# A hybrid decoder step on one core: TensorE's instructions issued strictly in the order of the source

## The chip, the cores and the metric

The kernel runs on one NeuronCore of a Trainium2 chip. The metric is the device time of one execution in microseconds. The kernel before takes 2900.02 us, the median of three runs.

## The reference

One inference step of a decoder of two layers, for 1104 tokens of width 1024: 16 meta tokens and 1024 prompt tokens of one sequence, and 8 sequences of 8 new tokens each with states of their own. All arithmetic is fp32.

```python
def trunk_layer(x, pos, lw, states, front_pad, chunk, attend):
    m, new_states = hybrid_mixer(rmsnorm(x, lw['g_pre_mix']), pos, lw, states, front_pad, chunk, attend)
    x = x + rmsnorm(m, lw['g_post_mix'])
    gate, up = jnp.split(rmsnorm(x, lw['g_pre_ffn']) @ lw['w_ffn_in'], 2, axis=-1)
    x = x + rmsnorm((jax.nn.silu(gate) * up) @ lw['w_ffn_out'], lw['g_post_ffn'])
    return x, new_states
```

`hybrid_mixer` multiplies the normed tokens by one input projection and hands its columns to three mixers: a gated DeltaNet (4 heads of 128 x 128 state, after a causal convolution of width 4), a Mamba-2 SSD scan (4 heads of 64, state 128), and sliding-window attention with sinks (4 query heads, window 128). Their outputs, 512 + 256 + 256 columns, are concatenated (`mixed`) and go through the output projection. The DeltaNet works in chunks: inside a chunk a triangular system is solved, and between chunks a state S is carried, in this recurrence:

```python
    def step(s, inp):
        u_c, w_c, attn_c, qd_c, kd_c, gl_c = inp
        v_new = u_c - jnp.einsum('bhcd,bhde->bhce', w_c, s)
        o_c = jnp.einsum('bhcd,bhde->bhce', qd_c, s) + jnp.einsum('bhij,bhje->bhie', attn_c, v_new)
        s = s * gl_c[..., None, None] + jnp.einsum('bhcd,bhce->bhde', kd_c, v_new)
        return s, o_c
```

## The kernel before

**Tiles.** The tokens lie in 9 tiles, eight of 128 and one of 80. Every dense product (input projection, output projection, feed-forward) is made of three fp16 matmuls: a weight slab `wsp` and the tokens (`xn`, `mixed` or `hsp`) are each split into a high and a low half, and high x high, high x low and low x high are added up in one PSUM bank (`mm3` and `mm3x`, lines 619 and 624). The loops run over layers, then over weight slabs or token tiles, then over 8 blocks of the contraction. The feed-forward takes part of its columns plainly and the rest by a product of 2 x 2 blocks with 7 instead of 8 multiplications.

**Stages of a layer.** Norm and transposes of the tokens (`norm_t`, line 586), the input projection, attention, SSD (`ssm_pre`, line 1844), the DeltaNet (`dn_inv`, line 1540, solves the triangular systems of four chunks at a time in two streams "0" and "1"; `dn_chain`, line 1680, is the recurrence; `dn_gate`, line 1794, gates its result into `mixed`), the output projection (in `dense`, line 831), the norm behind it with a second norm and its transposes (`out_post`, line 2026), and the feed-forward. All dense products of both layers are one generator, `dense`. Of the output projection, the three last tiles (6 to 8) are done in two parts, all heads but the last DeltaNet head first, with the part sums kept in DRAM; the tiles 0 to 5 are projected whole once the last head is done.

**The recurrence on the chip.** One chunk of `dn_chain` is a loop through three engines: a matmul of k and the state, `r` on VectorE (scalar_tensor_tensor out of PSUM), a matmul of `TF` and r, `y` on ScalarE (a copy out of PSUM), a matmul of `kd` and y, and the new state `S` on VectorE. Its matmuls are fp32; the trace shows each of them as two passes.

**`out_post`.** For a token tile it squares the projection's result `m` on ScalarE, multiplies m by a gain (VectorE or GpSimd, whichever the planner holds to be free first, `tt`, line 304), takes the root on GpSimd (`rqy`), adds to the residual `xt` on VectorE, stores it, and then does the same for the next norm, writing `m` again, whose eight 128 x 128 blocks TensorE transposes into the banks `tr` and `ch`. They are evicted into `xn2` for the feed-forward.

**What sets the order.** The source is one Python program in which each stage is a generator that yields where it must wait. The class `Plan` runs the generators. It wraps every engine (`engine`, line 206; the instruction itself is issued in line 214), and keeps a clock for each one. After each instruction `note` (line 155) adds the cost of a small table to that engine's clock:

```python
    HOP = {"T": 200.0, "V": 150.0, "S": 170.0, "G": 140.0, "D": 900.0}
    RATE = {"V": (1.04, 90.0), "S": (0.85, 55.0), "G": (2.1, 60.0)}
```

RATE is ns per column and a fixed part, HOP what is added before another engine may use a result; a matmul costs 0.42 ns (fp16) or 1.68 ns (fp32) per column and 3 ns. `run` (line 236) takes the first generator, by priority, whose operands are ready by that clock within 30 ns of TensorE's (`ready <= now + 30`), and emits its next instructions; the chains have priority 0, the inversions and norms 1, the dense products 9. So the source has a planned order of emission for all engines. PSUM is shared by tags: two banks `pd` and two `ps_inv`, two `ps_o`, one `ps_ch`, one `ps_tr`.

The emitted program then goes through the toolchain's scheduler. It keeps all dependencies, and chooses within them, by a timing model of its own, the order in which each engine issues; the order of emission is not binding for it. The number in an instruction's name is its place in the order of emission, so that the order on the chip can be laid beside it.

Of the kernel before, what the change touches and what calls it, by code (L numbers as in the profile page):

```python
# [110 lines left out]

NG = 23
NOW = -1.0


class Plan:
# [38 lines left out]
    def note(self, k, name, out, ins, acc, slow=False):  # L155
# [40 lines left out]
        if k != "D" or out.space != DRAM:  # L196
# [6 lines left out]
                L.append(b + (e + self.HOP[k],))  # L203
            self.last = max(self.last, e + self.HOP[k])

    def engine(self, eng, k):
        plan = self

        class E:
            def __getattr__(self, name):  # L210
                f = getattr(eng, name)

                def call(*a, **kw):
                    r = f(*a, **kw)  # L214
                    aps = [x for x in list(a) + [v for n, v in kw.items() if n not in ("out", "accum_out")]
                           if isinstance(x, bass.AP)]
                    out = kw.get("out")
                    if out is None:
                        out, aps = aps[0], aps[1:]
                    plan.note(k, name, out, aps, [kw["accum_out"]] if "accum_out" in kw else [],  # L220
                              kw.get("op") is ALU.pow)
                    return r

                return call

        return E()

    def mark(self, *keys):
        for key in keys:
            self.done[key] = self.last  # L230
# [5 lines left out]
    def run(self, *until):  # L236

        done = self.done
        while not until or any(k not in done for k in until):
# [31 lines left out]
            best[1], best[2] = self.last, None  # L271
            if r == NOW:
                best[1] = 0.0
# [8 lines left out]
def build(tc, A, depth=DEPTH):  # L282
    nc = tc.nc
    P = Plan()
    V, S, G, T, DQ = (P.engine(e, k) for e, k in ((nc.vector, "V"), (nc.scalar, "S"), (nc.gpsimd, "G"),
                                                 (nc.tensor, "T"), (nc.sync, "D")))
    dma = DQ.dma_start
    mark, done = P.mark, P.done
    es = ExitStack()
# [8 lines left out]
    def act(out, in_, func=AF.Copy, **k):  # L298
        S.activation(out=out, in_=in_, func=func, **k)
# [4 lines left out]
    def tt(out, a, b, op):  # L304

        n = 1
        for x in out.shape[1:]:
            n *= x
        t = {k: max(P.clk[k], P.clk["T"]) + P.RATE[k][0] * n for k in "VG"}
        (V if t["V"] <= t["G"] else G).tensor_tensor(out, a, b, op=op)  # L310
# [42 lines left out]
    def PS(tag):  # L353
        n = {"tr": 1, "inv": 2, "ch": 1, "o": 2}[tag]
        t = psm.tile([128, 512], F32, tag=tag, bufs=n, name="ps_" + tag)
        P.take(tag, n, t)
        return t
# [31 lines left out]
    def later(key, fn, n=0):  # L389

        def g():
            yield (key,)
            fn()
            free(n)
            mark((key, "st"))
        P.add(0, g())

# [13 lines left out]
    def load7(my, key, src):  # L411
# [11 lines left out]
        for k in range(4):  # L423
# [5 lines left out]
            def put(o, x):  # L429
                yield P.clk["V"]  # L430
                act(w[:, o, :512], x, scale=WS)
                stt(w[:, o, 512:], x, WS, w[:, o, :512], MUL, SUB)
# [20 lines left out]
            mark(key + (k,))  # L453
            yield NOW

# [6 lines left out]
    def loader():  # L462
        while True:
# [31 lines left out]
            if key[0] == "w2" and key[2] == 0:  # L495
# [3 lines left out]
                split[0] += 1  # L499
                yield NOW  # L500
                continue
# [29 lines left out]
            mark(key)  # L531
            yield NOW

# [52 lines left out]
    def norm_t(xt, C, i, gb, dst, xs, tag, halves=False):  # L586
# [6 lines left out]
        for hf in range(2):  # L593
# [13 lines left out]
            V.tensor_tensor(lo, pc, hi, op=SUB)  # L607
            yield NOW if hf == 0 else None

# [19 lines left out]
    def dense_ws(p, w, xn, g):  # L629

        g0, gn = g
        for kt in range(8):
            mm3(p[:, :gn], w[:, 0, kt * 128:(kt + 1) * 128], w[:, 1, kt * 128:(kt + 1) * 128],
                xn[:, kt, 0, g0:g0 + gn], xn[:, kt, 1, g0:g0 + gn], kt == 0, kt == 7)
            if kt < 7:
                yield NOW

# [1622 lines left out]
def make(arrays, depth=DEPTH):  # L2260
    import concourse.bacc as bacc

    nc = bacc.Bacc("TRN2", target_bir_lowering=False, num_devices=1)
    A = {n: nc.dram_tensor(n, a.shape, mybir.dt.from_np(a.dtype), kind="ExternalInput").ap()
         for n, a in arrays.items()}
    for n, s in OUTS.items():
        A[n] = nc.dram_tensor(n, s, F32, kind="ExternalOutput").ap()
    with tile.TileContext(nc) as tc:
        build(tc, A, depth)
    return nc  # L2270
# [9 lines left out]
```

## Time and profile before

| | us |
|---|---|
| median of 3 runs (2899.88 to 2901.44) | 2900.02 |
| the profiled execution | 2895.58 |
| its span, first to last instruction | 2893.5 |
| mean granted clock of TensorE in it | 0.981 |
| busy: TensorE / its weight loads | 2743.2 / 1909.5 |
| busy: VectorE / ScalarE / GpSimd | 1933.3 / 1288.4 / 813.1 |

The profiled execution is one execution with the hardware profiler on; 2.08 us of its time lie outside the span. Engines are named PE (TensorE's matmuls), PEld (its weight loads, which run beside the matmuls), DVE (VectorE), ACT (ScalarE), POOL (GpSimd) and SP (the queue of DMA issues). A busy time is the time in which at least one instruction of the engine runs. Nearly every instruction has the line 214, since the planner's wrapper issues it; so groups are told apart by the program's names, out<-in. The granted clock is a share of TensorE's full 2.4 GHz.

### The profile page before, as it was taken

What the parts mean: (1) busy time and instruction counts of PE and PEld (TensorE: products, weight loads), DVE (VectorE), ACT (ScalarE), POOL (GpSimd) and SP (SyncE); (2) the same over time, 40 slices, a digit from 0 to 9 for tenths busy, and PEclk for the clock granted to TensorE, in tenths of its full rate; (3) what the DMA queues carried; (4) which work ended last, traced back from release to release, by engine and by line L of the source; (5) the groups of instructions that cost most, each with busy time, mean ns of one, the idle gap of its engine ahead of it and who ended that gap; (6) DMA issues with size and microseconds to landing.
All of it is one profiled execution on the core that took longest, in us unless ns stands there. A gap on an engine that the chain in (4) does not pass through costs nothing. (4 is left out here: it accounts for less than half of the span.)

```text
span 2893.5 us, 50019 instructions
## 1 busy us (share of the span) xinstructions
PE 2743.2 (95%) x19662; PEld 1909.5 (66%) x19662; DVE 1933.3 (67%) x3614; ACT 1288.4 (45%) x3015; POOL 813.1 (28%) x1124
## 2 busy tenths in 40 slices
PE   6999999999799999999899999999998999999997
PEld 3766677664588888744348676777646888886443
DVE  5557667655757676767865676666457666766776
ACT  5435456554423333433544455655543333334342
POOL 2204523313543333200260062223136233231011
PEclk8999999999899999999999999999999999999998
DMA  5011110132301111242431111001222111113333
GB/s 183 31 60 37 57 38 31 38 104 89 109 30 59 53 51 59 96 120 68 163 128 34 50 47 46 31 31 56 86 103 87 50 54 59 52 52 110 106 115 124
DMA packets 74092, 209.79 MB, mean 73 GB/s; under 512 B 13360, under 2 KB 24816, under 8 KB 73824
## 3 DMA queue, kind: packets, MB, share of 16 engines
q1 hardware_dynamic: 73856, 206.59, 21.8%
q8 instruction: 154, 2.52, 0.4%
q14 instruction: 82, 0.67, 0.1%
HBM read 175.49 MB, written 33.04 MB: 72 GB/s over the span
## 5 line engine op out<-in xcount | busy, mean ns | idle before, releaser
L214 PEld LDWEIGHTS <-wsp 128*128 128x128 f16 x10704 | 1044.1, 99 | 305.7 <-issue 12.9
L214 PE MATMUL pd<-xn,wsp 128*128 128x336 f16 (+3 forms) x4512 | 737.7, 311 | 3.4 <-DVE a L214 3.1
L214 DVE SCALAR_TENSOR_TENSOR wsp<-raw,wsp 128x512 f16<-128x512 f32 (+2 forms) x414 | 404.8, 986 | 196.3 <-ACT wsp L214 193.5
L214 ACT ACTIVATE wsp<-raw 128x512 f16<-128x512 f32 (+2 forms) x414 | 311.0, 763 | 393.5 <-DVE raw L214 145.9
L214 PEld LDWEIGHTS <-hsp 128*128 128x128 f16 x1848 | 182.1, 99 | 242.0 <-issue 30.2
L214 PE MATMUL pd<-wsp,hsp 128*128 128x512 f16 x924 | 232.6, 385 | 17.1 <-ACT wsp L214 11.8
L214 PE MATMUL ps_o<-wsp,hsp 128*128 128x512 f16 x924 | 230.7, 383 | 0.5 <-DVE m L214 0.5
L214 PE MATMUL pd<-wsp,mixed 128*128 128x512 f16 (+1 forms) x864 | 212.0, 384 | 5.8 <-DVE m L214 5.8
L214 POOL TENSOR_SCALAR rqy<-ss 128x1 f32<-128x1 f32 (+1 forms) x72 | 56.1, 779 | 551.1 <-ACT jk L214 407.6
L214 DVE SCALAR_TENSOR_TENSOR u<-R,lp_cw,u 128x512 f32<-128x512 f32 x216 | 180.0, 869 | 4.3 <-ACT u L214 3.4
L214 ACT ACTIVATE hsp<-hid 128x512 f16<-128x512 f32 x154 | 89.8, 620 | 180.4 <-PE ps_o L214 143.7
L214 PE MATMUL pd<-wsp,xn 128*128 128x512 f16 (+3 forms) x864 | 161.2, 338 | 6.0 <-ACT wsp L214 3.4
L214 PE MATMUL ps_o<-xn,wsp 128*128 128x256 f16 (+1 forms) x1296 | 165.1, 285 | 0.0
L214 POOL TENSOR_TENSOR raw<-raw 128x512 f32<-128x512 f32 x74 | 95.5, 1292 | 241.9 <-DVE raw L214 208.4
L214 PE MATMUL ps_inv<-xn,wsp 128*128 128x256 f16 (+1 forms) x1248 | 154.0, 281 | 0.8 <-DVE a L214 0.8
L214 POOL TENSOR_TENSOR U<-U,hid 128x256 f32<-128x256 f32 (+1 forms) x114 | 80.3, 733 | 239.3 <-ACT hid L214 239.3
L214 PEld LDWEIGHTS <-mixed 128*128 128x128 f16 (+1 forms) x864 | 84.4, 101 | 82.4 <-issue 11.3
L214 DVE TENSOR_TENSOR hsp<-hid,hsp 128x512 f16<-128x512 f32 x154 | 101.4, 684 | 43.3 <-ACT hsp L214 43.3
L214 PEld LDWEIGHTS <-xn 128*128 128x128 f16 (+1 forms) x864 | 87.4, 103 | 55.9 <-issue 10.7
L214 PE MATMUL ps_ch<-xn,wsp 128*128 128x296 f16 x456 | 109.2, 289 | 0.0
L214 PE MATMUL ps_tr<-xn,wsp 128*128 128x256 f16 x456 | 108.6, 273 | 0.0
L214 DVE TENSOR_TENSOR W<-ps_inv,c 128x512 f16<-128x512 f32 (+1 forms) x120 | 71.0, 595 | 46.3 <-PE ps_inv L214 45.4
(496 smaller groups left out, 4738.9 us busy)
## 6 DMA issues: line engine op xcount, KB each, us to landing
raw<-wfi SPq DMA_DIRECT2D x88, 512.0 KB, 3.5
raw<-wfo SPq DMA_DIRECT2D x70, 512.0 KB, 3.7
raw<-wf SPq DMA_DIRECT2D x44, 512.0 KB, 3.3
xd<-xt SPq DMA_DIRECT2D x24, 512.0 KB, 2.9
xt<-xd SPq DMA_DIRECT2D x24, 512.0 KB, 5.7
xt<-x SPq DMA_DIRECT2D x16, 512.0 KB, 6.1
raw<-wo SPq DMA_DIRECT2D x16, 512.0 KB, 3.4
tcx<-wfo SPq DMA_DIRECT2D x10, 512.0 KB, 3.7
```

The lines of the kernel that those rows point to most:

```text
L214: r = f(*a, **kw)
```

## The change

The planner gets a method `keep`, which is called with each instruction that the wrapper has just issued and its engine's letter. For the letters in `PINNED`, here "T" alone, it hands the instruction to the toolchain's `keep_in_program_order`, which puts it in issue order behind the instruction of the same engine that was handed over before it. The edge holds inside one engine's queue: it adds no semaphore and no instruction. TensorE's 18392 matmuls and transposes are so issued in the order of emission. The other engines' instructions are ordered by the scheduler as before, with TensorE's order given.

```diff
--- before.py
+++ after.py
@@ -111,6 +111,7 @@
 
 NG = 23
 NOW = -1.0
+PINNED = "T"
 
 
 class Plan:
@@ -203,6 +204,10 @@
                 L.append(b + (e + self.HOP[k],))
             self.last = max(self.last, e + self.HOP[k])
 
+    def keep(self, k, ins):
+
+        return self.pin(ins) if k in PINNED else ins
+
     def engine(self, eng, k):
         plan = self
 
@@ -211,7 +216,7 @@
                 f = getattr(eng, name)
 
                 def call(*a, **kw):
-                    r = f(*a, **kw)
+                    r = plan.keep(k, f(*a, **kw))
                     aps = [x for x in list(a) + [v for n, v in kw.items() if n not in ("out", "accum_out")]
                            if isinstance(x, bass.AP)]
                     out = kw.get("out")
@@ -282,6 +287,7 @@
 def build(tc, A, depth=DEPTH):
     nc = tc.nc
     P = Plan()
+    P.pin = tc.keep_in_program_order
     V, S, G, T, DQ = (P.engine(e, k) for e, k in ((nc.vector, "V"), (nc.scalar, "S"), (nc.gpsimd, "G"),
                                                  (nc.tensor, "T"), (nc.sync, "D")))
     dma = DQ.dma_start
```

## Rows read from the trace of the kernel before

**Rows 1.** The page, part 1: busy us, share of the span, instructions.

```profile
PE 2743.2 (95%) x19662; PEld 1909.5 (66%) x19662; DVE 1933.3 (67%) x3614; ACT 1288.4 (45%) x3015; POOL 813.1 (28%) x1124
```

**Rows 2.** Waits of TensorE, whole span: us in total, times, longest us.

```profile
PE ps_tr L214 <- DVE m L214: 31.2, 15, 6.7
```

**Rows 3.** Windows, all engines: window, us, busy (count) by engine, PEclk, DMA share, GB/s.

```profile
10.00:75.00 65.00, 47.28 (x244) 26.33 (x242) 35.22 (x56) 32.96 (x77) 21.84 (x36) 0.84 0.48 162
647.00:683.10 36.10, 33.18 (x200) 20.90 (x198) 16.14 (x49) 14.69 (x57) 10.27 (x15) 1.00 0.19 61
1398.80:1493.40 94.60, 81.77 (x388) 38.34 (x388) 79.68 (x100) 46.95 (x78) 35.56 (x44) 0.97 0.48 154
```

**Rows 4.** TensorE's timeline at the chain's end: start us, us, what it did.

```profile
656.34 0.59 PE L214 MATMUL pd<-wsp,mixed 128*128 128x512 f16 x2
656.77 0.44 PE L214 MATMUL ps_ch<-r,TF 128*128 128x128 f32 x2
...
672.69 0.38 PE L214 MATMUL pd<-wsp,mixed 128*128 128x512 f16 x1
...
681.00 2.32 PE L214 MATMUL pd<-wsp,mixed 128*128 128x512 f16 x10
```

**Rows 5.** Tiles y and r, whole span: duration in ns, min/median/max.

```profile
L214 PE MATMUL ps_ch<-y,prep x144: 270/275/377, 403.0 to 2100.9; 128*128 128x128 f32 x128, 16*128 16x128 f32 x16
...
L214 ACT ACTIVATE y<-ps_ch x72: 254/277/322, 402.5 to 2100.4; 128x128 f32<-128x128 f32 x64, 80x128 f32<-80x128 f32 x8
...
L214 DVE SCALAR_TENSOR_TENSOR r<-ps_ch,nE,prep x80: 332/348/353, 401.6 to 2099.2; 128x128 f32<-128x128 f32 x64, 64x128 f32<-64x128 f32 x8, 16x128 f32<-16x128 f32 x8
```

**Rows 6.** Timelines of VectorE and GpSimd, 748 to 765 us.

```profile
755.06 3.36 DVE L214 SCALAR_TENSOR_TENSOR xt<-m,rqy,xt 128x1024 f32<-128x1024 f32 x1 [2.10 <-POOL rqy L214]
...
761.52 1.28 DVE L214 SCALAR_TENSOR_TENSOR m<-xt,rqy,gpf 128x1024 f32<-128x1024 f32 x1 [0.72 <-POOL rqy L214]
...
754.98 2.35 POOL L214 TENSOR_TENSOR m<-m,gpo 128x1024 f32<-128x1024 f32 x1
```

**Rows 7.** Windows, tile pd alone: window, us, busy (count) of PE, DVE, ACT, PEclk, ...

```profile
647.00:683.10 36.10, 15.32 (x53) 0.00 (x0) 1.68 (x4) 1.00 0.19 61
2070.40:2106.50 36.10, 15.33 (x53) 0.00 (x0) 1.67 (x4) 1.00 0.19 61
450.20:465.20 15.00, 7.61 (x37) 0.00 (x0) 0.55 (x3) 1.00 0.11 37
```

**Rows 8.** TensorE's timeline around the output projection's end and after.

```profile
752.01 1.75 PE L214 MATMUL ps_o<-xn,wsp 128*128 128x256 f16 x8
...
759.07 1.56 PE L214 MATMUL pd<-wsp,mixed 128*80 128x512 f16 x6 [2.92 <-DVE m L214]
...
763.41 0.75 PE L214 MATMUL ps_tr<-c,m 128*128 128x128 f32 x4
...
781.42 0.37 PE L214 MATMUL pd<-xn,wsp 128*128 128x256 f16 x1 [3.15 <-DVE a L214]
784.65 1.09 PE L214 MATMUL ps_tr<-c,m 128*128 128x128 f32 x4 [2.86 <-DVE m L214]
```

**Rows 9.** Groups by form, TensorE, 752.0 to 784.6 us: busy, mean, idle before.

```profile
L214 PE MATMUL ps_o<-xn,wsp 128*128 128x256 f16 x48 | 8.1, 335 | 0.0
L214 PE MATMUL pd<-xn,wsp 128*128 128x256 f16 x49 | 6.3, 275 | 3.1 <-DVE a L214 3.1
L214 PE MATMUL ps_inv<-xn,wsp 128*128 128x256 f16 x48 | 5.4, 272 | 0.0
```

**Rows 10.** TensorE's timeline at the start of an inversion.

```profile
607.54 2.97 PE L214 MATMUL pd<-wsp,mixed 128*128 128x512 f16 x13
611.20 0.40 PE L214 MATMUL ps_inv<-c,Mh 128*128 128x128 f16 x4 [0.69 <-ACT Mh L214]
```

**Rows 11.** Windows, all engines, columns as in rows 3: the clock after two waits.

```profile
2203.90:2210.70 6.80, 2.64 (x13) 2.34 (x14) 5.38 (x7) 3.45 (x7) 2.43 (x4) 0.52 0.60 202
...
760.10:763.50 3.40, 3.40 (x17) 2.31 (x16) 2.59 (x3) 1.89 (x4) 3.13 (x4) 0.53 1.01 334
```

## Prediction

> **What bounds the kernel now.** I read the page first: TensorE is busy for 2743.2 of the span's 2893.5 us [rows 1]. It is the bound over the run, and the 150.3 us in which it stands idle are what an order of its instructions can add to or take from. Next came the list of what it waits for: transposes that wait for a VectorE result `m` lead with 31.2 us in 15 waits, the longest of 6.7 us [rows 2]. The reader should see that no single wait is large: the leading kind is a sum of short pauses.
>
> Then I put two orders side by side: the one in which the source emits the matmuls, and the one in which the program before has them. Of 18392 matmuls 2472 stand elsewhere, none by more than 101 places: 1110 further forward, 1362 further back. The displaced ones form 92 closed stretches. In them 949 dense matmuls (a weight slab as one operand) run ahead of work that the source emits first; their spacings add up to 189 us. I sorted the idle time before each matmul the same way: 13.6 us of it ends at one that was moved forward, 58 us at one moved back, 67 us at one that was not moved. So little of today's waiting is the fault of a matmul that went too early, and the dense work moved forward mostly fills time in which the earlier work was not ready.
>
> The page's rows by window say the same for the stretches that matter [rows 3]: TensorE is busy for 33.18 of 36.10 us at the end of the DeltaNet chain, and for 81.77 of 94.60 us between the layers. The timeline shows how: in the chain's end each step of the recurrence (S, r, y) leaves TensorE a pause, and two dense matmuls sit in it [rows 4].
>
> **What the change does to that.** It adds no work on any engine and no wait between engines; it takes away the freedom to fill. A matmul whose operands are late now holds up everything emitted behind it. How late they are follows from the source: the planner emits a step where its own cost table says that it is ready. The table gives 109 + 55 = 164 ns for the 128-column copy to y on ScalarE, the row says 277; 133 + 90 = 223 ns for r on VectorE, the row says 348 [rows 5]. It gives VectorE's 1024-column pass 1155 ns, and the row shows 3.36 us where GpSimd's pass on m runs beside it [rows 6]. So the emitted order is too early for the steps that wait, and TensorE pays the difference. Four places in each layer, named by layer 0:
>
> *Chain end, 647.0 to 683.1 us.* The output projection of the first tiles is emitted only when the planner has the last head's result, behind the whole chain. Its first matmuls need the other three heads alone, so the program before runs 53 of them here (the only tile pd has in this window, and 53 again in layer 1) [rows 7]. Ten of them in a row take 2.32 us [rows 4]; less the 0.38 that one takes to drain this is 0.216 each, so 11.4 us of work moves behind the chain. The chain itself gains little: its steps start within 0.1 us of their operands already. I take 10.5 us. Ends: 8.5 if the 2.9 us of idle time here go as well; 16 if the emptier stretch runs at half clock (the 48 chain passes of the y, r and S kinds at 0.377 instead of 0.275 us [rows 5] add some 5).
>
> *Output projection to FFN, 752 to 789 us.* The source emits the transposes of tile 5 right behind the projection of tile 6, which ends at 752.0; they start at 763.41 [rows 8], because the VectorE and GpSimd passes in front of them end only then [rows 6]. Before, dense matmuls of the FFN go in between. Up to the transposes of tile 7 at 784.65 [rows 8], 144 of them have run (48 + 49 + 48 [rows 9], less the one after the 3.15 us wait); the source emits 72 ahead of these transposes. The other 72 at 0.1125 us (5.4 us for 48) are 8.1 us. Besides, tile 7's projection moves from between 752.0 and 759.07 to behind 764 [rows 8], and its eviction on VectorE by up to 6.5 us; most of that is absorbed by VectorE's queue, I add 1. Taken: 9. Ends: 2 if the 3.15 and 2.86 us of waiting there [rows 8] vanish; 15 if the delay passes on in full.
>
> *Two inversion streams, 450 to 488 us.* 62 matmuls of 384 columns are moved forward, 37 of them before 465 [rows 7]. At 0.164 us (384 at the rate of 512 columns in 0.216) that is 10.2 us. Two streams cover part of each other's waits, so I take 4; ends -1.4 (the idle time of the stretch) and 10.2.
>
> *Start of an inversion, 605 to 614.5 us.* The source has it wait for Mh, which is there at 611.2; 13 dense matmuls fill the time now [rows 10]. By the two orders 27 are moved forward here, 5.8 us. I take 4; ends -0.7 and 5.8.
>
> The smaller stretches of a layer hold another 91 such matmuls, 15 to 20 us at these spacings, with some 7 us of idle time. There the source is early by a fraction of a microsecond at a time and the filler comes right behind; I take 0, with ends -7 and 20. Four places in two layers: 2 x (10.5 + 9 + 4 + 4) = 55 us.
>
> Once only: between the layers (1398.8 to 1493.4) 90 matmuls, 22 us, are moved forward and 12.8 us are idle [rows 3]. VectorE is busy for 79.68 of 94.60 us, so it sets the pace either way: 5 us, ends -11 and 22. At the end of layer 1, 35 matmuls, 9 us: 2 us, ends 0 and 9. In the first 75 us, 88 matmuls, 19 us at full clock, stand against 65.00 - 47.28 = 17.7 us of idle time [rows 3]; loads and the norm chain hold both orders up: 0, ends -18 and 19.
>
> The sum is 55 + 5 + 2 + 0 = 62 us. The profiled execution takes 2895.58 us, its span 2893.5; 62 on top give 2957.6. It lies 4.4 us under the median of 2900.02, so against the median I forecast 2962 us. VectorE, ScalarE, GpSimd and the DMA queue keep their instructions; what they do later they do because a matmul came later, and that is inside the terms above.
>
> **The clock.** After the 2.92 us wait of 759 us the granted clock is 0.53 for a stretch of 3.4 us, after the 6.7 us wait of layer 1 it is 0.52 for 6.8 us [rows 2, 8, 11]: the lower level, 1.2 GHz, after an idle TensorE. The long waits that I expect stand where such drops already are, so the sum has nothing for it and the upper end holds it. The Trainium skill, "TensorE: Matmul & The Clock Gate", section "Loop structure matters more than you think", says that waits between matmuls let the array fall to the slow clock and that dense work should follow without gaps. By that rule three new long waits per layer would each cost some 2 to 3 us more of slow matmuls, an estimate from the page's two rates, and the sum would be near 78 instead of 62. By that rule the drops behind the waits of 2.92 and 6.7 us are what it describes, and these rows agree with it.
>
> **Rivals.** *Faster:* the five pauses that end at a matmul moved forward go, 13.6 us together, among them the one of 3.15 us at 781.4 [rows 8] and four of 1.4 to 3.4 us at the start and between the layers; the late chains lose the dense matmuls in front of them. That is 2886 us. It decides if the fill lost in the four places stays under 13.6 us, less than a quarter of what I count. For it speaks that the start and the seam between layers are such places; against it, that 53 matmuls alone are 11 us per layer. Chance 0.12.
>
> *Half of it:* the toolchain orders the other engines anew around the fixed TensorE order, so that VectorE and GpSimd serve the waiting transposes first; the pass of 3.36 us next to GpSimd's [rows 6] shows that there is room. Then the chain end (21 us) and a little more remain: 2926 us. Chance 0.20.
>
> *No change:* the edges order only what was in order, or gains at the seams and losses in the chains cancel: 2900 us. 2472 displaced matmuls speak against the first. Chance 0.10.
>
> *More:* every filler is lost and the clock falls as well, 2 x (16 + 15 + 10 + 6) = 94, with the seams, start and end over 100: above 3000 us. Chance 0.05.
>
> **How the numbers follow.** The forecast, 2940 to 3000 with 2962 in it, has 0.53. A measurement of this kernel can tell about 0.2%, 5.8 us, from no change. Slower by more: 0.53 + 0.20 + 0.05 = 0.78; within: 0.10; faster: 0.12. The range 2894 to 3000 leaves out the faster case and the one above, 0.17 together.
>
> **What would show it.** In the changed profile the chain's end should hold no matmul of the output projection, with TensorE busy for some 22 us instead of 33.18. The transposes of m should lead the list of waits with pauses near 10 us at tile 5, and a pause of about 4 us should stand before the first matmul on Mh. TensorE's idle time should come to about 212 us, its busy time stay within 10 us of 2743. If the idle time falls, or the transposes of m wait less, the forecast is wrong in its direction; if it grows only at the chain's end, it was half of it.

## The result, and the profile after

The changed kernel takes 3014.53 us (median of 4 runs, 3011.94 to 3018.61) against 2899.95 us (4 runs): a ratio of 1.0398, 95% interval 1.0385 to 1.0411, slower by 114.6 us. The direction of the forecast holds; the time does not. 2962 was forecast, and 3014.53 lies above the range's end of 3000.

The page after, part 1, answers to [rows 1]:

```profile
PE 2782.6 (92%) x19662; PEld 1940.3 (64%) x19662; DVE 1933.8 (64%) x3614; ACT 1291.6 (43%) x3015; POOL 818.3 (27%) x1124
```

Its span is 3010.1 us, 116.6 more than before. TensorE executes the same instructions, yet is busy for 39.4 us more (2782.6 against 2743.2), and stands idle for 3010.1 - 2782.6 = 227.5 us, 77.2 more than the 150.3 of before. Those are two losses, and the split is the main reading of this case. The mean granted clock went from 0.981 to 0.960. As the clock has two levels, full and half, these means stand for about 110 us at half clock before and about 241 us after, an estimate from the two spans.

Where they arise is seen by taking points at which both kernels have executed the same set of matmuls, and comparing the windows between them. Ten such windows, five in each layer, hold 99.1 of the 116.6 us. Here are those of layer 0 and the sum over all ten, first of the kernel before (the chain's end is in [rows 3]; columns as there, the sum line has the ten windows' lengths first):

```profile
450.20:487.70 37.50, 36.10 (x318) 28.06 (x316) 25.63 (x62) 24.03 (x70) 9.92 (x19) 1.00 0.13 44
505.80:548.20 42.40, 39.17 (x318) 27.30 (x316) 29.26 (x58) 22.76 (x53) 10.64 (x21) 0.96 0.16 52
605.00:611.40 6.40, 5.71 (x38) 3.10 (x37) 4.99 (x8) 2.21 (x3) 1.27 (x2) 1.00 0.52 165
...
751.40:788.70 37.30, 28.02 (x201) 22.10 (x200) 31.00 (x33) 15.16 (x29) 23.20 (x24) 0.84 0.39 130
...
sum 319.40, PE 283.91 PEld 202.91 DVE 213.79 ACT 157.95 POOL 110.75; mean PE 28.39 PEld 20.29 DVE 21.38 ACT 15.79 POOL 11.08
```

And of the kernel after:

```profile
451.10:496.40 45.30, 41.69 (x313) 33.52 (x313) 25.40 (x62) 23.98 (x68) 9.85 (x18) 0.81 0.10 36
514.70:562.70 48.00, 41.11 (x318) 28.94 (x317) 30.63 (x59) 22.74 (x53) 10.84 (x19) 0.89 0.14 46
620.40:630.80 10.40, 7.00 (x37) 3.96 (x38) 7.52 (x11) 3.26 (x4) 1.28 (x2) 0.84 0.57 182
666.80:722.30 55.50, 42.67 (x195) 26.94 (x195) 19.16 (x53) 17.02 (x58) 10.09 (x15) 0.78 0.21 71
790.20:836.40 46.20, 29.41 (x202) 22.33 (x201) 34.55 (x45) 18.28 (x37) 31.62 (x31) 0.76 0.29 98
...
sum 418.50, PE 327.17 PEld 233.65 DVE 242.14 ACT 172.61 POOL 131.70; mean PE 32.72 PEld 23.36 DVE 24.21 ACT 17.26 POOL 13.17
```

The count behind TensorE's busy time hardly changes from one to the other (318 and 313 entries in the first window), the busy time does, and the clock column says why. In the ten windows TensorE is busy for 327.17 - 283.91 = 43.3 us more and idle for 55.8 us more. Place by place, each growth as busier + idler:

| place | layer 0 | layer 1 | taken in the sum |
|---|---|---|---|
| two inversion streams | 7.8 = 5.6 + 2.2 | 6.5 = 4.1 + 2.4 | 4 |
| 505.8 to 548.2 us | 5.6 = 1.9 + 3.7 | 5.3 = 1.6 + 3.7 | 0 |
| start of an inversion | 4.0 = 1.3 + 2.7 | 5.3 = 2.6 + 2.7 | 4 |
| chain's end | 19.4 = 9.5 + 9.9 | 21.2 = 11.2 + 10.0 | 10.5 |
| projection to feed-forward | 8.9 = 1.4 + 7.5 | 15.1 = 4.1 + 11.0 | 9 |

Outside them the seam between the layers adds 5.4 us and the end of layer 1 4.7 us. The first 75 us end 0.8 us later, after a detour: 9.0 us are lost there and won back.

The leading wait of TensorE is the same as before [rows 2], and the one that is now second has grown from 10.9 to 23.0 us (columns as there):

```profile
PE ps_tr L219 <- DVE m L219: 42.8, 14, 11.3
PE ps_tr L219 <- DVE xt L219: 23.0, 4, 9.1
```

Its two longest stand where the forecast put "pauses near 10 us at tile 5". The one in layer 0, in the timeline (start us, us, what it did):

```profile
787.97 0.60 PE L219 MATMUL ps_ch<-c,m 128*128 128x128 f32 x4
788.40 2.63 PE L219 MATMUL pd<-wsp,mixed 128*128 128x512 f16 x6
801.20 1.08 PE L219 MATMUL ps_tr<-c,m 128*128 128x128 f32 x4 [10.17 <-DVE m L219]
```

### The profile page after: what moved, and what is told of

The parts are those of the page before. It is cut to its first block, busy times and chain, and to the rows that moved or that the text cites. A ratio compares the mean times of both kernels' runs of the same rounds, so it can differ in the third digit from the quotient of the medians.

```text
span 3010.1 us, 50030 instructions
## 1 busy us (share of the span) xinstructions
PE 2782.6 (92%) x19662; PEld 1940.3 (64%) x19662; DVE 1933.8 (64%) x3614; ACT 1291.6 (43%) x3015; POOL 818.3 (27%) x1124
## 5 line engine op out<-in xcount | busy, mean ns | idle before, releaser
L219 PE MATMUL ps_tr<-xn,wsp 128*128 128x256 f16 x456 | 108.6, 273 | 0.0
```

Of the source, the lines that this page charges most:

```text
L219: r = plan.keep(k, f(*a, **kw))
```

## The experiments

All start from the changed kernel. Each was timed beside the kernel before on the same chip; the table has the difference of the medians, and, from its profiled execution, TensorE's busy and idle time (the span less the busy time) and its mean granted clock.

| run | median us | to before | busy | idle | clock |
|---|---|---|---|---|---|
| before | 2900 | 0 | 2743.2 | 150.3 | 0.981 |
| changed | 3014.5 | +114.6 | 2782.6 | 227.5 | 0.960 |
| two_orders | 2923.3 | +25.6 | 2744.2 | 176.2 | 0.979 |
| free_out | 2951.9 | +51.4 | 2755.0 | 193.5 | 0.973 |
| free_inv | 2973.2 | +74.4 | 2768.9 | 204.0 | 0.968 |
| early | 3013.2 | +115.6 | 2770.6 | 239.9 | 0.960 |
| load | 3003.5 | +103.0 | 2778.3 | 220.6 | 0.964 |
| early_load | 2972.3 | +71.7 | 2767.2 | 206.7 | 0.966 |
| dummy | 3024.1 | +126.4 | 2796.5 | 226.0 | 0.964 |
| dummy2 | 3009.1 | +108.6 | 2791.8 | 218.0 | 0.967 |
| hop | 3002.1 | +104.5 | 2768.7 | 229.2 | 0.962 |
| all_pinned | 3014.5 | +115.7 | 2780.3 | 232.9 | 0.956 |
| early_load_free | 2892.8 | -6.0 | 2745.2 | 147.3 | 0.978 |
| early_free | 2902.7 | +3.2 | 2747.0 | 153.0 | 0.979 |

**Which order costs.** In `two_orders` the ordering edges tie dense matmuls only to dense ones and the rest only to the rest:

```diff
-    P.pin = tc.keep_in_program_order
+    prev = {}
+
+    def pin(ins):
+        side = P.cur == "dense"
+        if side in prev:
+            tc.add_manual_dep(ins.ins, prev[side].ins.name, mybir.DependencyInfo(
+                mybir.DependencyClass.NoSync, mybir.DependencyReason.DATA), reason="keep_in_program_order")
+        prev[side] = ins
+        return ins
+
+    P.pin = pin
```

(`P.cur` is the name of the generator that the planner runs.)

> The dense matmuls keep the source's order among themselves, and all other TensorE instructions keep it among themselves, but the one kind is free against the other. If the 114.6 us are lost because dense work may no longer run ahead of chains and transposes (the theory), nearly all of it comes back: 2895 to 2925 us. If the loss lies in the order of the chains, inversions and transposes among themselves (the rival), it stays above 2960 us.

2923.26 us: 89 of the 114.6 us come back. TensorE's busy time is within 1 us of the kernel before, the clock at 0.979: with the dense work free, the whole of the clock's loss is gone. The 25.6 us that stay are idle time (176.2 against 150.3); the order inside either kind is all that is still bound.

**Is the loss where the windows say?** Two runs bind everything but the dense matmuls of one stage: `free_out` those from the part sums of the output projection to the first plain products of the feed-forward, `free_inv` those from the DeltaNet's projections to the part sums.

```diff
+    def pin(ins):
+        if P.free and P.cur == "dense":
+            return ins
...
+            P.free = True
             part = range(NT - NPT, NT)
```

> Order of the source everywhere, but the dense matmuls from the output projection to the first plain products of the feed-forward are free against the rest. By the growth of the changed kernel between common points (19.4 and 21.1 us at the chain's end, 8.9 and 13.6 us from the output projection to the feed-forward) the theory expects 63 us back, 2947 to 2957 us. If the loss is spread by something else than these places (the rival), above 2980 us.

> Order of the source everywhere, but the dense matmuls from the DeltaNet's projections to the part sums of the output projection are free against the rest; those of the output projection's whole tiles and all later ones are bound. By the growth of the changed kernel between common points in the inversions (18.9 and 19.7 us from the first chain to the last head) the theory expects 39 us back and some 2 us per layer more from the last tile's part sums, 2970 to 2978 us. If the inversions are late by their own order against the chain and not by the lost fill (the rival), over 2995 us.

2951.93 and 2973.15 us: 63.2 and 40.2 us come back (the four runs of `free_inv` lie between 2961.86 and 2976.87). The sum, 103.4 of 114.6 us, counts one place twice: the dense matmuls at the start of an inversion are part sums of the output projection, which both runs leave free, and the 4.0 and 5.3 us lost there are gone in both. So some 94 us come back from distinct places, against 99.1 in the ten windows; in `free_out` the chain's end still loses 3.9 and 3.8 us. The freed matmuls are not tied to one another either. The pages, part 1, of `free_out` and of `free_inv`:

```profile
PE 2755.0 (93%) x19662; PEld 1930.3 (65%) x19662; DVE 1934.6 (66%) x3614; ACT 1290.6 (44%) x3015; POOL 814.4 (28%) x1124
```

```profile
PE 2768.9 (93%) x19662; PEld 1925.4 (65%) x19662; DVE 1930.4 (65%) x3614; ACT 1289.3 (43%) x3015; POOL 820.6 (28%) x1124
```

Of the busy time 27.6 us come back in the one and 13.7 in the other, 41.3 together, where 39.4 were lost; of the idle time 34.0 and 23.5. Here too the start of an inversion is counted in both.

**What the filler in the chain is worth.** Here the order stays bound and the source is changed: it emits the three-heads part of the first tile's projection before it asks for the last head (not shown: `dense_tok` gets two arguments, so that one call can begin a sum and a later one finish it).

```diff
+            yield tuple(("mix", l, h, 0) for h in range(3)) + (("ssm", l, 0), ("swa", l, 0))
+            early = []
+            for hf in range(2):
+                early.append(pd())
+                yield from dense_tok(early[hf], mx, wo[hf * 4:hf * 4 + 4], 0, 512, (0, 1, 2, 4, 5, 6, 7), True, False)
+                yield NOW
             yield room(2)
...
-                    p = pd()
+                    p = early[hf] if i == 0 else pd()
```

> Order of the source as in the changed kernel, but the source emits the three-heads part of the output projection's first tile, 42 matmuls, as soon as three heads are done, so that the planner puts it into the last chain's pauses. Theory that the fill is what is lost: 42 x 0.216 = 9.1 us per layer come back from the moved work alone, 2996 us; with the clock that falls in the emptied chain some 6 us per layer more, 2980 to 2988 us. Rival, that the chain is late by its own order: over 3008 us.

3013.24 us, no change: over 3008, as the rival had it, but not for its reason. The fill worked, TensorE's busy time fell by 12.0 us. A new wait ate it, seen in the timeline behind the chain:

```profile
706.86 0.37 PE L219 MATMUL ps_tr<-c,on 80*128 80x80 f32 x1 [2.06 <-DVE on L219]
707.02 2.77 PE L219 MATMUL pd<-wsp,mixed 128*128 128x512 f16 x6
720.94 1.09 PE L219 MATMUL ps_tr<-c,m 128*128 128x128 f32 x4 [11.15 <-DVE m L219]
```

The planner put the first tile's transposes straight behind the 6 matmuls that finish its projection; in the changed kernel 84 dense matmuls stand ahead of them. TensorE waits 11.15 us for the norm in front of them. The cause lies in the planner: a load counts in the `last` of the generator that issues it, so that a projection was held to be unready until the load of its residual `xt` is in, which it does not read. One line takes that away:

```diff
                 dma(xt[:C], (A["x"] if L.first else xd[2 * l - 1])[i * 128:i * 128 + C, :])
+                P.last = P.clk["T"]
```

> Order of the source as in the changed kernel, but the planner no longer counts the loads of m and xt as something that the next projection has to wait for (one line sets its time back to TensorE's clock behind them), so that the source emits dense matmuls ahead of the transposes of tiles 4 to 7. Theory that the waits of 10.2 us (layer 0) and 11.3 us (layer 1) for m come from the place in which the source puts those transposes: 8 to 12 us per layer come back, 2990 to 3000 us. Rival, that VectorE and GpSimd set the pace of the norm behind the projection whatever TensorE's order is: over 3006 us.

> The first tile's 42 matmuls in the last chain's pauses, as in the run before it of that name, and the planner's wait for the loads gone, so that the first tile's transposes are no longer emitted 6 matmuls behind its projection (where TensorE waited 11.15 us for them). Theory that the emptied chain costs its fill and its clock: 9 to 15 us per layer under the run with the loads' wait alone gone, 2962 to 2982 us. Rival, that work moved into the chain is lost again to the norm behind the projection: within 6 us of that run.

`load` alone takes 3003.54 us, between the theory and its rival: 11 us better than the changed kernel, not 16 to 24. In layer 0 the wait of 10.17 us has become one of 3.34 and one of 8.86 us. Between points that both kernels share, from behind the chain to the feed-forward (before: 683.8 to 789.9 us, and 2107.0 to 2214.0), layer 0 is shorter by only 1.6 us (113.05 against 114.65) and layer 1 by 11.7 us (109.04 against 120.74), though the wait of 11.33 us there is still 9.94. So the place of the transposes in the source is part of the loss, and most of the long wait stays: the norm on VectorE and GpSimd in front of it is itself late. Why the two layers differ so much is open. Layer 0 in the timeline:

```profile
788.34 2.72 PE L219 MATMUL pd<-wsp,mixed 128*128 128x512 f16 x6 [3.34 <-DVE m L219]
799.93 1.08 PE L219 MATMUL ps_tr<-c,m 128*128 128x128 f32 x4 [8.86 <-DVE m L219]
```

`early_load` takes 2972.27 us, 31.3 us under `load`, 15.6 us per layer for 42 x 0.216 = 9.1 us of work. The stall behind the chain is gone:

```profile
713.71 15.28 PE L219 MATMUL pd<-wsp,mixed 128*128 128x512 f16 x60
728.83 0.60 PE L219 MATMUL ps_tr<-c,m 128*128 128x128 f32 x4
```

Between the profiled executions of those two, busy time falls by 11.1 us and idle time by 13.9. So matmuls that fill a pause were worth more than their own time here. The clock is part of it: its mean rises from 0.964 to 0.966, some 14 us less at half clock, which can account for about 7 of the 11.1 us, an estimate from the spans. What made the rest is not shown.

**The clock by itself.** `dummy` adds spare matmuls behind the last head's chain matmuls, into unread columns of the same bank (and changes nothing that is read); `fill` is called behind each of a chunk's three chain matmuls:

```diff
+            def fill(p):
+                if h == 3:
+                    for _ in range(2):
+                        P.pin(nc.tensor.matmul(p[:, 128:512], lhsT=id16, rhs=L.mixed[0][:, 0, 0:384],
+                                               start=True, stop=True))
```

> Order of the source as in the changed kernel, and in the last head's chain two spare fp16 matmuls of 384 columns behind each of its three matmuls per chunk, 52 per layer, into columns that nobody reads. The chain's end grew by 19.4 and 21.1 us, of which 53 x 0.216 = 11.4 us is dense work that moved behind it. Theory: most of the rest, 8 to 10 us per layer, is the half clock (0.71 to 0.84 granted there), which spare work would prevent: 2995 to 3005 us, with a granted clock of 0.98 or more from the chain's start to its end. Rival: the rest is waits that the strict order makes, whatever the clock; then the spare matmuls, 52 x 0.16 = 8.3 us per layer, are hidden at best and on the path at worst: 3012 to 3031 us.

3024.05 us, slower by 9.5 us than the changed kernel, although the clock is held, at 1.00 and then 0.99 in layer 0 and at 1.00 and then 0.92 in layer 1 (windows of `dummy` in layer 0, columns as in [rows 3]):

```profile
670.00:694.00 24.00, 19.72 (x122) 13.02 (x122) 7.87 (x25) 7.70 (x33) 3.85 (x7) 1.00 0.09 29
694.00:709.00 15.00, 10.52 (x64) 6.78 (x63) 3.61 (x12) 4.20 (x17) 3.72 (x5) 0.99 0.12 36
```

The timeline says why. The copy to y on ScalarE is released by the spare matmul (L1699) and not by the chain's own one, so the spare work lay on the path:

```profile
683.71 0.49 PE L1699 MATMUL ps_ch<-mixed,c 128*128 128x384 f16 x2
684.29 0.28 ACT L219 ACTIVATE y<-ps_ch 128x128 f32<-128x128 f32 x1 [3.69 <-PE ps_ch L1699]
```

The Trainium skill, "PSUM — Partial Sum Buffer", section "PSUM bank collisions raise a hardware error", says that the compiler's back end makes any two instructions of different engines depend on each other that touch the same 32-partition quadrant of a bank. By that rule the copy has to wait for matmuls into other columns, and the trace agrees: the copy is released by the spare matmul, and the shortest chunks of the chain take 3.97 us here. `dummy2` gives the spare matmuls a bank of their own (`z`, a tile of tag "d" for each chunk):

```diff
+            def fill(z):
+                for _ in range(2):
+                    P.pin(nc.tensor.matmul(z, lhsT=id16, rhs=L.mixed[0][:, 0, 0:512], start=True, stop=True))
```

> Order of the source as in the changed kernel, and spare matmuls again behind each of the last head's chain matmuls, two of 512 columns, now into a bank of their own that nobody reads, so that no result waits for them. Theory that part of the chain's end is the half clock: granted 0.98 or more there, the chain from its first to its last y 30 to 31 us instead of 33.1 and 34.2, the dense matmuls behind it at 0.216 instead of 0.26 us: 4 to 6 us per layer, 3002 to 3007 us. Rival, that the clock costs nothing because the chain waits for VectorE and ScalarE: 3012 us or more.

3009.08 us, between theory and rival: 5 us better. The chain itself answers: 31.7 and 31.0 us from the first to the last y instead of 33.1 and 34.2, and its shortest steps are near 2.95 us. But in layer 0 the chain starts 3.8 us later than in the changed kernel, before the first spare matmul, and behind the chain the clock falls nonetheless (0.81 in 690 to 709 us, 0.67 in 709 to 724). As a test of the total it is inconclusive: what the spare work itself costs was not separated from what the clock gives.

**The planner's table.** `hop` sets what the planner adds before another engine may use a result to 275, 285 and 230 ns for VectorE, ScalarE and GpSimd:

```diff
-    HOP = {"T": 200.0, "V": 150.0, "S": 170.0, "G": 140.0, "D": 900.0}
+    HOP = {"T": 200.0, "V": 275.0, "S": 285.0, "G": 230.0, "D": 900.0}
```

> Order of the source as in the changed kernel, with one size changed: what the planner adds before another engine may use a result of VectorE, ScalarE and GpSimd goes from 150, 170 and 140 to 275, 285 and 230 ns, by the durations that the trace shows (348 ns where the table has 223, 277 where it has 164). Theory that the emitted order is too early for the steps that wait: of the some 34 us lost in the inversions (450 to 548 and 605 to 614 us of each layer) half or more comes back, and some of the chain's end, 2975 to 3000 us. Rival, that the times in the table do not matter and it is the rule of who goes first: within 6 us of 3014.5.

3002.13 us, 12.4 us better and just outside the theory's range. It was no clean test: the planner now starts the first chain 19.5 us later, the last head's chain takes 39.5 us instead of 33.1, and 72 operations moved from VectorE to GpSimd. That the table is too optimistic is shown by [rows 5]; how much of the loss it makes is open.

**The other engines.** `all_pinned` has `PINNED = "TVSG"`.

> The change made for TensorE, VectorE, ScalarE and GpSimd alike. Theory that TensorE's order alone is what costs, and the other engines' order matters little because they follow it: 3000 to 3030 us. If the toolchain's order of the other engines does not fit a TensorE bound to the source (a rival), the source's order on all four is under 2990 us. If the toolchain's freedom on the other three engines softens the change much (the rival of the prediction that would halve it), over 3040 us.

3014.45 us, the changed kernel's time to 0.1 us. With TensorE bound, the scheduler's freedom on the other three engines is worth nothing in sum here. The prediction's rival "half of it" rested on that freedom, and falls.

**The two edits with nothing bound.** Both edits of the source, that of `early` and that of `load`, with no engine bound (`PINNED = ""`), and then the first of them alone:

> The two edits of the source that helped the bound order (the first tile's 42 matmuls emitted in the last chain, the loads' wait gone), with no engine bound, as in the kernel before. Theory that the toolchain's scheduler did both by itself: 2890 to 2905 us, no change against the kernel before. If a better order of emission also guides the scheduler (the rival), 2870 to 2888 us.

> The kernel of the last run (no engine bound) with one of its two edits alone: the first tile's 42 matmuls emitted in the last chain, the loads' wait as before. If the some 6 us come from this edit, 2889 to 2896 us; if they come from the loads' wait, 2896 to 2903 us, as the kernel before, since the scheduler puts these matmuls into the chain by itself.

2892.79 us, ratio 0.9974 (0.9963 to 0.9985) to the kernel before: a small gain, inside the theory's range and short of the rival's. The first edit alone is 1.0009 (1.0000 to 1.0018). So the first edit gives the free scheduler nothing, which fits the theory that it fills the chain by itself, and what it gains from is the loads' edit, alone or with the other; that edit without the other and nothing bound wasn't tried.

## Why the prediction was wrong

**What held.** The four places and their filler were right, and the waits named came: the transposes of m at tile 5 after 10.17 and 11.33 us ("near 10"), no output projection in the chain's end, Mh waited for (2.92 us, "about 4"). As idle time the two large terms were close: the chain's end 9.9 and 10.0 (10.5 taken), projection to feed-forward 7.5 and 11.0 (9). The two small ones came to little more than half: the start 2.7 twice (4), the two streams 2.2 and 2.4 (4). The idle time should have come to about 212 us; it came to 227.5. That the total is so near is in part luck: the small terms fell short by 6 us, and 505.8 to 548.2 us, taken at 0, added 7.4. `two_orders`, `free_out` and `free_inv` show that the lost freedom of the dense matmuls in these places is the cause.

**The step that failed: the clock.** The prediction read the drops to half clock [rows 11] as something that follows a long wait, reasoned that "the long waits that I expect stand where such drops already are, so the sum has nothing for it", and expected TensorE's busy time "within 10 us of 2743". It grew by 39.4 us, and the time at half clock more than doubled, from about 110 to about 241 us by the mean clocks. The clock does not fall only behind long waits: it fell in stretches that were merely thinned. In the chain of layer 0 TensorE is busy for 3.83 of 6.80 us, with no pause over 1.44 us, and the next 7.2 us are granted 0.50 (windows of the changed kernel, columns as in [rows 3]):

```profile
670.00:676.00 6.00, 4.28 (x31) 3.50 (x31) 1.79 (x7) 2.32 (x9) 0.87 (x2) 1.00 0.00 1
676.00:682.80 6.80, 3.83 (x26) 2.94 (x24) 2.04 (x7) 3.12 (x15) 2.84 (x5) 0.99 0.01 2
682.80:690.00 7.20, 6.66 (x23) 4.81 (x24) 2.82 (x9) 1.88 (x7) 0.50 (x2) 0.50 0.26 74
```

Over the chain's end, without any output projection in it (667.1 to 708.8 us, granted 0.77), TensorE was busy for 29.1 us, where the prediction expected some 22. Before, the same chain had 33.18 of 36.10 us filled and ran at 1.00 [rows 3]. Here is what the lower clock does to it, in the timeline of `ps_ch<-y,prep`, one per chunk:

```profile
674.70 0.49 PE L219 MATMUL ps_ch<-y,prep 128*128 128x128 f32 x2 [1.14 <-ACT y L219]
...
677.47 0.49 PE L219 MATMUL ps_ch<-y,prep 128*128 128x128 f32 x2 [0.43 <-ACT y L219]
...
681.46 0.49 PE L219 MATMUL ps_ch<-y,prep 128*128 128x128 f32 x2 [1.44 <-ACT y L219]
...
685.28 0.79 PE L219 MATMUL ps_ch<-y,prep 128*128 128x128 f32 x2 [0.43 <-ACT y L219]
...
689.51 0.80 PE L219 MATMUL ps_ch<-y,prep 128*128 128x128 f32 x2
...
693.25 0.79 PE L219 MATMUL ps_ch<-y,prep 128*128 128x128 f32 x2 [0.43 <-ACT y L219]
```

The same two passes take 0.49 and then 0.80 us, and a chunk of five steps without other work, 2.77 us from 674.70, start to start, becomes 3.74 from 689.51. (The chunk from 685.28, 4.23 us, holds four transposes besides.) The chunk from 677.47, 3.99 us, is at full clock: there the copy to y stands behind ScalarE's copies out of four transposes, which the source emits in one piece, and behind squares `jk`; in the kernel before, the transposes stand as three and one and the squares in another chunk. So the chain is longer by 5.1 us in layer 0 and 6.2 in layer 1, where the prediction took nothing for it. The clock is not all of that. In layer 0, 2.2 us arise in two chunks at full clock (3.75 and 3.99 us instead of 2.78 and 2.72) and 2.3 us in two at half clock (4.23 and 3.74 instead of 2.90 and 2.77). Behind the chain the clock costs too, as the 55 dense matmuls that follow it up to 723 us take 14.3 us, 0.26 each instead of 0.216.

The upper end of the chain's term was 16, with 5 for the clock; the place measured 19.4 and 21.2. That end counted the clock for the chain's passes of the y, r and S kinds only, neither for the other matmuls of the chain nor for the dense ones behind it. The two inversion streams, with ends up to 10.2, were granted 0.81 (layer 1: 0.85) instead of 1.00; more than half of their growth is busy time.

The Trainium skill, "TensorE: Matmul & The Clock Gate", section "Loop structure matters more than you think", says that a long wait between matmuls lets the array go cold. By that rule the prediction had a sum of 78 beside its 62, for three new long waits per layer. The trace agrees with the direction, and shows the same fall without a long wait, which the estimate had no place for.

In the profiled spans the growth of 116.6 us is the 62 us forecast, 39.4 us of busy time that the sum had nothing for, and 15.2 us by which the forecast idle time was too small.

**Smaller misses.** The smaller stretches were taken at 0, though their filler was counted at 15 to 20 us per layer; 505.8 to 548.2 alone lost 5.6 and 5.3. The argument that "the filler comes right behind" was wrong there. The seam was 5 and measured 5.4; the end of layer 1 was 2 and measured 4.7; the first 75 us, taken at 0, 0.8. The 0.164 us of the inversion streams' matmuls should be 0.162 by the rate given for it, 0.1 us in that term.

**The rivals.** "Faster": the five pauses in front of matmuls moved forward do go in part (the first 75 us win back 8 us between 60.7 and 74.7), but other waits come ahead of them. "Half of it" fell by `all_pinned`. "More", at 0.05, is what came, with the fill and the clock lost together; it added 94 and the seams. It deserved more than that chance: in all ten windows TensorE is both busier and idler, so the two losses came together.

## What to carry to other kernels

Count a lost filler twice: once as idle time, and once for the clock of the work that stays in the thinned stretch and of what follows it, by the durations of the same matmuls at full and at half clock in the trace. Split any change of the time into busy and idle time before looking for waits; where the same instructions are busy for longer, no list of waits shows it. An order written out by a planner with a cost table is only as good as the table and its rules of readiness; the loads' rule was a hidden wait that a free scheduler had mostly covered (with nothing bound, both edits together gave 6 us).

## What the runs showed of the hardware

The granted clock fell to 0.50 in a chain without a pause over 1.44 us, and also behind waits of 0.55, 0.56 and 1.49 us in the inversions, where it then stayed at 0.50 for 14 us although TensorE was busy for 13.48 of them (windows of the changed kernel, columns as in [rows 3]):

```profile
451.10:456.00 4.90, 2.61 (x25) 2.02 (x25) 4.42 (x8) 4.65 (x9) 0.04 (x1) 0.80 0.28 92
456.00:462.00 6.00, 5.80 (x37) 5.43 (x36) 2.22 (x6) 1.41 (x4) 0.00 (x0) 0.50 0.04 16
462.00:470.00 8.00, 7.68 (x33) 4.29 (x31) 6.02 (x13) 3.49 (x6) 3.41 (x5) 0.50 0.24 78
```

So no long wait was needed here. With spare matmuls between its steps the same chain kept 1.00 for 24 us. And matmuls into unread columns of a bank held up the engine that reads other columns of it, as the program was compiled: 3.97 us for the shortest chunks against some 2.95 with a bank of their own.
